# Attention's values as seven products of halves, with tokens on partitions and most moving parts kept on chip

## The chip, the core and the metric

The kernel runs on one core of a Trainium2 chip. The metric is device time in microseconds, the median over runs; one more execution is recorded by the profiler, and its time is given beside the median. The engines are called PE (TensorE), DVE (VectorE), ACT (ScalarE), POOL (GpSimd) and SP (SyncE).

## What is computed

One layer over 512 tokens of width 2048, in float32. A normalised input `h = rmsnorm(x)` is multiplied by a wide matrix; the columns of the product are queries, keys, values and gates of two mixers:

```python
h = rmsnorm(x, norm_gain)
proj = h @ w_in
(aq, ak, av, az, iq, ik, iw, rq, rk, rv, rz, ga, gb) = split(proj)
a_out = dsa_mixer(aq, ak, av, iq, ik, iw, positions, rel_bias) * silu(az)     # top-k attention, 8 heads of 128
b_out = retention_mixer(rope(rq), rope(rk), rv, ret_gn_gain) * silu(rz)       # 8 heads of 128
merged = sigmoid(ga) * (a_out @ w_a_out) + sigmoid(gb) * (b_out @ w_b_out)
r = x + merged @ w_o
y = rmsnorm(r + (p @ w_ple) * sigmoid(r @ w_ple_gate), final_gain)
```

The change is in `av`, the values of the attention: 512 tokens x 1024 columns, a sum over 2048.

## The kernel before

The order of all work is written out by hand: one Python program issues instructions to the engines' queues, and a queue runs in the order in which it was filled. What is wanted later is put off with `later(n, f)`, by `n` ticks of `step()`, a call that stands behind every few matmuls. `todo` holds work for the next ticks, and `bg` work for the background, of which one item is taken every `state["rate"]` ticks when `todo` is empty.

A float32 operand is used as two parts, high and low: ACT rounds the high part (`L137` for weights), DVE subtracts it for the low part (`L142`). A product takes three matmuls: high x high, high x low, low x high.

Weights arrive through `raw` (a DMA of 512 KB into one of seven `wraw` buffers) and `units` (one split into `wh` and `wl`, three buffers of each). `split_to` and `load_to` run ahead of the matmuls by `AHEAD` = 3 and `LOADS` = 5 units more. Most projections are computed in pairs by `gemm_pair`: two outputs of 128 channels, the sum over 2048 cut in two halves, tokens cut in two halves, so that seven products of half blocks replace eight (the scheme of Strassen in Winograd's form). Its seven weight combinations come from DMAs that add to a buffer (`add_block`, on POOL's queue) and one addition on DVE (`L144`). Its seven moving combinations, `PRODUCTS` = s3, a11, a12, s4, s2, a22, s1, have eight row blocks each: 56 tiles of 128 x 512 (256 high and 256 low columns). `combos` builds them, four steps for each row block `k`; a step rounds on ACT and subtracts on DVE. The 56 tiles are built in the background, stored to `hd` in memory, and loaded back later.

The stages that matter here, in order:

- The index scores, whose queries are the first projection. Row block 0 of the moving parts is begun here.
- `values(u_rv[i], "rv")`, retention's values: tokens are on the output's partitions, `hparts` (32 tiles: 16 row blocks of `h` in two parts) are the stationary operand, and weights of 512 columns move. Each of the two calls has 16 row blocks x 4 token tiles x 3 matmuls. In the background, at one item in two ticks, the moving parts are built.
- `values(u_av[i], "av")`, attention's values, in the same form, with the weights in 16 units of two row blocks. In the background are the 48 top-k rounds (`MAX8` and `MATCH_REPLACE8` on DVE), one in three ticks. Here `x_load` brings the 56 tiles back, while `hparts` are freed. The result is scaled by `R["nat"]`, split and stored to `vd`.
- 24 gate pairs: eight retention heads, each one `gemm_pair` for its query and key and two for gates. In the background, at one item in 18 ticks, are the masks of the position bias.
- The pairs of the other projections, attention, the output projections and the end.

On chip, 69 tiles of 128 x 512 (`U`), five of 128 x 1280 (`B`) and eight PSUM banks (`P`) are handed out.

Of the kernel before, what the change touches and what calls it, by code (L numbers as in the profile page):

```python
# [35 lines left out]
def block_kernel(tc, xT, pT, posb, posq, w_in, w_v, w_ik, w_a, w_b, w_o, w_ple, w_gate,  # L36
# [4 lines left out]
    with contextlib.ExitStack() as ctx:  # L41
# [10 lines left out]
        def U(name, dt=F32):  # L52
            return up.tile([128, L], dt, name=name, tag="u")
# [17 lines left out]
        raw_tiles = {}  # L71
        unfinished = {}
        state = {"raw": 0, "split": 0, "rate": BG_RATE}
        in_raws = set()

        def raw(src, k0, nk, cols, plus=None):
            raws.append((src, k0, nk, cols, plus))
# [2 lines left out]
        def block(src, chunks, cols=128):  # L80
            ids, k0 = [], 0
            for nk in chunks:
                ids.append(len(units))
                units.append((raw(src, k0, nk, cols), None, nk, cols))
                k0 += nk
            return ids

        def block_pair(s1, s2):
# [8 lines left out]
                units.append((r, plus, 8, 128))  # L97
            return list(range(first, first + 7))

        def view(t, nk, cols):  # L100
            return t.rearrange("p a c -> p (a c)")[:, 0:nk * cols].rearrange("p (a c) -> p a c", c=cols)

        def add_block(r, b):
            src, k0 = b
            pool.dma_start(out=raw_tiles[r], in_=src[:, k0:k0 + 8, :], accum_op=OP.add)  # L105
# [53 lines left out]
        def later(n, f):  # L159
            if n <= 0:  # L160
                return f()
            tick[1] += 1
            heapq.heappush(soon, (tick[0] + n, tick[1], f))
# [108 lines left out]
                if ended[n] == 16 and n in after:  # L272
                    after[n]()

        def combos(lo, hi, name, keep=None):


            X = {n: [None] * 8 for n in PRODUCTS}
            T = {}

            def parts(n, k, src, sign=1.0):
                t = U(name + n, F32R)
                act.activation(t[:, LO], src, AF.Copy, scale=sign)
                if sign > 0:
                    dve.tensor_sub(t[:, HI], src, t[:, LO].bitcast(F32))
                else:
                    dve.scalar_tensor_tensor(t[:, HI], src, sign, t[:, LO].bitcast(F32), op0=OP.mult, op1=OP.subtract)
                if keep is None:
                    X[n][k] = t
                else:  # L290
                    later(6, lambda: sp.dma_start(keep(n, k), t.bitcast(F32)))
# [33 lines left out]
        u_rv, u_av = ([block(w_v[i], (2,) * 8, 512) for i in g] for g in ((0, 1), (2, 3)))  # L325
        u_r, u_g = [], []
        for h in range(NH):
            u_r.append(block_pair(col(RQ, h), col(RK, h)))
# [345 lines left out]
            for b, ps in [(b, bias_mm(b)) for b in banks]:  # L674
                bias_out(b, ps)

        hd = dp.tile([56, 128, L], F32, name="hd")
        x_at = {(n, k): hd[8 * i + k] for i, n in enumerate(PRODUCTS) for k in range(8)}
        xn = {}

        def xn_load(k):
# [178 lines left out]
        Xh = {n: [None] * 8 for n in PRODUCTS}  # L860
        x_wanted = collections.deque((n, k) for n in PRODUCTS for k in range(8))

        def x_load(count):
            while x_wanted and count:
# [3 lines left out]
                count -= 1  # L868

        for i in range(2):  # L870
            for t, ps in enumerate(values(u_rv[i], "rv")):
                act.dma_start(rd[i, t], normal(ps, "rv", t))
        for i in range(2):
            pss = values(u_av[i], "av", lambda s, i=i: x_load(2 if i else 1 + s % 2))
            vs = [normal(ps, "av", t, F32 if t == NT - 1 else F32R) for t, ps in enumerate(pss)]
            for t in range(NT - 1):
                vl = U("avl", F32R)
                dve.scalar_tensor_tensor(vl, pss[t], R["nat"][:, t:t + 1], vs[2 * t].bitcast(F32), op0=OP.mult,
                                         op1=OP.subtract)
                vs.insert(2 * t + 1, vl)  # L880
            for j, v in enumerate(vs):
                later(8 + (6 if i else 2) * j, lambda v=v, j=j, i=i: act.dma_start(vd[i, j], v if j == 6 else v.bitcast(F32)))
# [30 lines left out]
        state["rate"] = BG_RATES[3]  # L913
        for n, u in enumerate(u_rz):
            y = B("y2")

# [402 lines left out]
AHEAD = 3  # L1319
LOADS = 5  # L1320
BG_RATE = 4
BG_RATES = (2, 3, 18, 9)
HEAD = 13
WARM = 10
MANUAL = True
# [96 lines left out]
```

## Time and profile before

| what | value |
|---|---|
| median of three runs | 1683.71 us (1683.71 to 1684.24) |
| the profiled execution | 1684.08 us, of which the span is 1682.3 us |
| granted TensorE clock | 0.998 |
| PE, weight loads, DVE, ACT, POOL busy | 99%, 86%, 76%, 51%, 13% of the span |
| DMA | 355.85 MB, 212 GB/s over the span |
| values of retention | from 95.7 us; of attention, from 192.1 to 279.1 us |

In the profile, a group of instructions is shown by its line, its engine and operation, what it writes and reads, how often it ran, its busy time and the mean of one in ns, and then the idle time of the engine just before it and what ended that. PEld are the weight loads of PE. A matmul's end is modelled, and matmuls overlap.

### The profile page before, as it was taken

To read this page: it belongs to the slowest core of one execution; us is meant where nothing else is said; L and a number is where in the kernel's file an instruction comes from. 1 tells how busy PE (TensorE), PEld (TensorE's weight loads), DVE (VectorE), ACT (ScalarE), POOL (GpSimd) and SP (SyncE) were. 2 spreads that over 40 slices of the span, in tenths; PEclk is the share of its full clock that TensorE was granted. 3 is DMA by queue.
4 is the path that set the end of the run, shared out by engine and by line. 5 is a ranking of instruction groups with operands and counts; after the bars stand their busy time and mean duration, and the time that the engine had idled before them with its cause. 6 is when DMAs were issued, how large, how long until landed. Compare 5 with 4: busy or idle time off the path is not lost.

```text
span 1682.3 us, 24757 instructions
## 1 busy us (share of the span) xinstructions
PE 1669.6 (99%) x9208; PEld 1450.9 (86%) x9208; DVE 1275.8 (76%) x2020; ACT 864.8 (51%) x1278; POOL 216.4 (13%) x216
## 2 busy tenths in 40 slices
PE   9999999999999999999999999999999999999997
PEld 7988888888888888888888888888888888888896
DVE  7797888988888888877877876787668877864453
ACT  7465423555565555555555555566634444463342
POOL 2100000111111111111331111100000111112222
PEclk9999999999999999999999999999999999999999
DMA  7438989788788788788988888998566788733222
GB/s 289 126 107 308 374 296 337 176 228 218 187 225 207 200 215 212 199 213 212 254 237 221 214 206 232 242 361 292 173 202 191 194 224 214 209 112 100 88 63 100
DMA packets 135368, 355.85 MB, mean 212 GB/s; under 512 B 14800, under 2 KB 26960, under 8 KB 135248
## 3 DMA queue, kind: packets, MB, share of 16 engines
q1 hardware_dynamic: 102496, 256.20, 44.4%
q0 software_dynamic: 21376, 77.60, 25.4%
q10 hardware_dynamic: 11376, 20.47, 3.3%
q8 instruction: 72, 1.18, 0.3%
q14 instruction: 48, 0.39, 0.1%
HBM read 301.26 MB, written 52.95 MB: 211 GB/s over the span
## 4 chain that ended last, share of the span: by engine, by line
PE 95%; DVE 2%; ACT 1%; issue 1%; DMA 0%; POOL 0%; SPq 0%; POOLq 0%; DVEq 0%; ACTq 0%
PE ps_p L267 24%; PE ps_v L267 16%; PE ps_r L267 8%; PE ps_q L267 8%; PE ps_vn L734 3%; PE ps_vn L735 3%; PE ps_vn L736 3%; PE ps_w L198 3%; PE ps_w L197 3%; PE ps_w L199 3%; PE ps_pg L199 3%; PE ps_pg L197 3%; PE ps_pg L198 3%; PE ps_iq L197 1%; PE ps_iq L199 1%; PE ps_iq L198 1%
## 5 line engine op out<-in xcount | busy, mean ns | idle before, releaser
L142 DVE TENSOR_TENSOR wl<-wraw,wh 128x1024 fp32r<-128x1024 f32 (+2 forms) x459 | 560.0, 1231 | 186.3 <-ACT wh L137 184.3
L137 ACT ACTIVATE wh<-wraw 128x1024 fp32r<-128x1024 f32 (+2 forms) x459 | 474.4, 1043 | 305.4 <-DVE wraw L144 133.8
L105 POOL DMA_DIRECT2D wraw<-w_in x120 | 106.1, 957 | 833.7 <-DVE wl L142 262.5
L230 ACT ACTIVATE e<-ps_p 128x512 f32<-128x512 f32 x144 | 86.1, 598 | 146.9 <-PE ps_p L267 142.4
L267 PE MATMUL ps_p<-hs,wh 128*128 128x512 f32 x640 | 161.3, 394 | 0.0
L267 PEld LDWEIGHTS ps_p<-hs,wh 128*128 128x128 f32 x640 | 114.9, 189 | 21.2 <-issue 0.7
L734 PE MATMUL ps_vn<-wh,hh 128*128 128x512 f32 x256 | 99.8, 390 | 0.0
L735 PE MATMUL ps_vn<-wl,hh 128*128 128x512 f32 x256 | 99.7, 390 | 0.0
L736 PE MATMUL ps_vn<-wh,hl 128*128 128x512 f32 x256 | 99.7, 389 | 0.0
L267 PE MATMUL ps_p<-hs,wl 128*128 128x256 f32 x640 | 92.0, 284 | 0.0
L267 PEld LDWEIGHTS ps_p<-hs,wl 128*128 128x128 f32 x640 | 83.0, 192 | 0.5 <-issue 0.4
L267 PE MATMUL ps_v<-ha,wh 128*128 128x512 f32 x320 | 80.6, 393 | 0.0
L267 PE MATMUL ps_q<-ha,wh 128*128 128x512 f32 x320 | 80.1, 392 | 0.0
L267 PE MATMUL ps_r<-hs,wh 128*128 128x512 f32 x320 | 79.2, 389 | 0.4 <-ACT wh L137 0.4
L267 PE MATMUL ps_v<-hs,wh 128*128 128x512 f32 x320 | 79.5, 390 | 0.0
L267 PE MATMUL ps_p<-ha,wh 128*128 128x512 f32 x320 | 79.2, 390 | 0.0
L199 PE MATMUL ps_pg<-rh,wl 128*128 128x512 f32 x192 | 74.8, 390 | 0.0
L197 PE MATMUL ps_pg<-rh,wh 128*128 128x512 f32 x192 | 74.7, 389 | 0.0
L198 PE MATMUL ps_pg<-rl,wh 128*128 128x512 f32 x192 | 74.7, 389 | 0.0
L895 DVE TENSOR_TENSOR go<-e_t 128x256 f32<-128x256 f32 x160 | 68.0, 425 | 5.6
L267 PEld LDWEIGHTS ps_r<-hs,wh 128*128 128x128 f32 x320 | 60.0, 188 | 13.3 <-ACT wh L137 0.8
L267 PEld LDWEIGHTS ps_p<-ha,wh 128*128 128x128 f32 x320 | 60.0, 188 | 12.9 <-issue 0.4
(361 smaller groups left out, 3500.5 us busy)
## 6 DMA issues: line engine op xcount, KB each, us to landing
wraw<-w_in SPq DMA_DIRECT2D x172, 512.0 KB, 5.5
wraw<-w_in POOLq DMA_DIRECT2D x120, 512.0 KB, 8.0
wraw<-w_v SPq DMA_DIRECT2D x32, 512.0 KB, 4.9
wraw<-w_o SPq DMA_DIRECT2D x32, 512.0 KB, 5.0
wraw<-w_o POOLq DMA_DIRECT2D x24, 512.0 KB, 6.1
wraw<-w_gate SPq DMA_DIRECT2D x24, 512.0 KB, 3.9
hd<-hs SPq DMA_DIRECT2D x32, 256.0 KB, 4.9
hs<-hd SPq DMA_DIRECT2D x32, 256.0 KB, 5.4
```

Source lines behind the costliest of these rows:

```text
L105: pool.dma_start(out=raw_tiles[r], in_=src[:, k0:k0 + 8, :], accum_op=OP.add)
L137: act.activation(h, raw, AF.Copy)
L142: dve.tensor_sub(l, raw, h.bitcast(F32))
L197: pe.matmul(o, h[:, k, w], a, start=(s == order[0]), stop=False)
L198: pe.matmul(o, h[:, k, w], b, start=False, stop=False)
L199: pe.matmul(o, l[:, k, w], a, start=False, stop=(s == order[-1]))
L230: act.activation(E[n], src, AF.Copy)
L267: pe.matmul(o[:, c], w[:, k], X[PRODUCTS[n]][k][:, c], start=(n < 4 and first and k == 0), stop=(ended[n] == 16), skip_group_check=True)
L734: pe.matmul(pss[t], a[:, tok(t)], h[:, k], start=(s == 0), stop=False)
L735: pe.matmul(pss[t], a[:, tok(t)], l[:, k], start=False, stop=False)
L736: pe.matmul(pss[t], b[:, tok(t)], h[:, k], start=False, stop=(s == KT - 1))
L895: dve.tensor_add(o[:, q], c0, c1)
```

## The change

Attention's values take the form of `gemm_pair`, but with tokens on the output's partitions. The moving combinations become the stationary operand, 128 tokens at a time (columns `tok(j)` hold a high part, `tok(2 + j)` its low part), and the weight combinations move, 512 columns wide. The two outputs are the two blocks of 512 channels. Each of the seven products has eight row blocks x 2 token tiles x 3 matmuls, and the four accumulators take two banks each, all eight.

The weight combinations come from `block_wide_pair`: 20 loads, 16 adds by DMA on POOL's queue, 28 splits. The four `t` tiles lie in `B` buffers, and their first add is put off by 12 ticks.

The moving combinations must therefore be ready before attention's values, and 44 of the 56 stay on chip from when they are built. Twelve (s2, a22 and s1 of row blocks 0 to 3, `X_AWAY` = 4) are still stored and loaded back, now during retention's second call. The sums of `combos` and three of the low parts (s1, s4, a22) are issued on POOL instead of DVE; for the merged tiles later in the kernel, `combos` stays on DVE. The results of the values are not scaled any more, since the moving parts are normalised already.

The background's rates change: one item in five ticks during attention's values, one in 24 for what is left of the top-k rounds in the gate pairs, then one in 16, and later one in eight instead of nine.

```diff
+        def block_wide_pair(s1, s2):
+            ks = range(0, 8, 2)
+            t = [raw(s2, k, 2, 512, (s2, k + 8)) for k in ks]
+            w11, w21, w22 = ([raw(s, k + o, 2, 512) for k in ks] for s, o in ((s1, 0), (s1, 8), (s2, 8)))
+            s = [raw(s1, k, 2, 512, (s2, k)) for k in ks]
+            in_big.update(t)
+            first = len(units)
+            for r, plus in ((t, (s1, 0)), (w11, None), (w21, None), (w22, None), (t, (s1, 8)), (t, None), (s, None)):
+                units.extend((r[n], plus and (plus[0], plus[1] + k), 2, 512) for n, k in enumerate(ks))
+            return [list(range(i, i + 4)) for i in range(first, first + 28, 4)]
...
+                elif i in in_big:
+                    t = B("wt").rearrange("p (a c) -> p a c", c=128)
...
-                    add_block(i, plus)
+                    later(12 if i in in_big else 0, lambda i=i, plus=plus: add_block(i, plus))
...
-        def combos(lo, hi, name, keep=None):
+        def combos(lo, hi, name, keep=None, adder=dve, low={}):
...
-                    dve.tensor_sub(t[:, HI], src, t[:, LO].bitcast(F32))
+                    low.get(n, dve).tensor_sub(t[:, HI], src, t[:, LO].bitcast(F32))
...
-                dve.tensor_sub(t2[:, LO], x[:, LO], x[:, HI])
-                dve.tensor_sub(t1[:, LO], x[:, HI], y[:, HI])
-                dve.tensor_sub(t1[:, HI], x[:, LO], t1[:, LO])
-                dve.tensor_sub(t2[:, HI], y[:, LO], t1[:, HI])
+                adder.tensor_sub(t2[:, LO], x[:, LO], x[:, HI])
+                adder.tensor_sub(t1[:, LO], x[:, HI], y[:, HI])
+                adder.tensor_sub(t1[:, HI], x[:, LO], t1[:, LO])
+                adder.tensor_sub(t2[:, HI], y[:, LO], t1[:, HI])
...
-        _, h_step = combos(lambda k: xn[k], lambda k: xn[k + 8], "h", lambda n, k: x_at[n, k])
+        Xh, h_step = combos(lambda k: xn[k], lambda k: xn[k + 8], "h", lambda n, k: x_at.get((n, k)), pool,
+                            {n: pool for n in ("s1", "s4", "a22")})
...
+        bg.append(lambda: state.update(rate=BG_RATES[4]))
...
-        for i in range(2):
-            pss = values(u_av[i], "av", lambda s, i=i: x_load(2 if i else 1 + s % 2))
...
+        def value_out(i, t, f, x, y):
+            a = U("av")
+            f(a, x, y)
+            if t == NT - 1:
+                vs = [(6, a)]
+            else:
+                h, l = split(a, "av", 2)
+                vs = [(2 * t, h.bitcast(F32)), (2 * t + 1, l.bitcast(F32))]
+            for j, v in vs:
+                later(10 + 2 * (j % 2), lambda j=j, v=v: act.dma_start(vd[i, j], v))
...
+            after = {
+                0: lambda: copy("pv", "v"),
+                1: lambda: copy("e1", "p"),
+                2: lambda: out(dve.tensor_sub, "q", "e1", 0, 0),
+                4: lambda: copy("e2", "p"),
+                5: lambda: out(dve.tensor_sub, "v", "e2", 0, 1),
+                6: last,
+            }
+            for n, b in enumerate("vpqrpvp"):
...
+                for s, (i, k) in enumerate(seq):
+                    if k == 0:
+                        split_to(i + AHEAD)
+                        load_to(i + AHEAD + LOADS)
+                    h, l = loaded[i]
+                    x = Xh[PRODUCTS[n]][s]
+                    for j in range(2):
+                        a, c = x[:, tok(j)], x[:, tok(2 + j)]
+                        o = banks[b][j]
+                        pe.matmul(o, a, h[:, k], start=(n < 4 and s == 0), stop=False, skip_group_check=True)
+                        pe.matmul(o, a, l[:, k], start=False, stop=False, skip_group_check=True)
+                        pe.matmul(o, c, h[:, k], start=False, stop=(s == 7), skip_group_check=True)
+                        step()
+                if n in after:
+                    after[n]()
...
-BG_RATES = (2, 3, 18, 9)
+BG_RATES = (2, 3, 5, 24, 16, 8)
+X_AWAY = 4
```

More of the change, by code (lines that the diff above doesn't have):

```diff
@@ L73, in block_kernel @@
         state = {"raw": 0, "split": 0, "rate": BG_RATE}
-        in_raws = set()
+        in_raws, in_big = set(), set()
         def raw(src, k0, nk, cols, plus=None):
@@ L104, in add_block @@
             src, k0 = b
-            pool.dma_start(out=raw_tiles[r], in_=src[:, k0:k0 + 8, :], accum_op=OP.add)
+            _, _, nk, cols, _ = raws[r]
+            pool.dma_start(out=view(raw_tiles[r], nk, cols), in_=src[:, k0:k0 + nk, :], accum_op=OP.add)
         def load_to(n):
@@ L284, in parts @@
                 if sign > 0:
-                    dve.tensor_sub(t[:, HI], src, t[:, LO].bitcast(F32))
+                    low.get(n, dve).tensor_sub(t[:, HI], src, t[:, LO].bitcast(F32))
                 else:
                     dve.scalar_tensor_tensor(t[:, HI], src, sign, t[:, LO].bitcast(F32), op0=OP.mult, op1=OP.subtract)
-                if keep is None:
+                dst = keep and keep(n, k)
+                if dst is None:
                     X[n][k] = t
                 else:
-                    later(6, lambda: sp.dma_start(keep(n, k), t.bitcast(F32)))
+                    later(6, lambda: sp.dma_start(dst, t.bitcast(F32)))
             def sums(k):
@@ L324, in block_kernel @@
         u_iq = [None, None] + [block(col(IQ, m), K8) for m in range(2, 8)]
-        u_rv, u_av = ([block(w_v[i], (2,) * 8, 512) for i in g] for g in ((0, 1), (2, 3)))
+        u_rv = [block(w_v[i], (2,) * 8, 512) for i in range(2)]
+        u_av = block_wide_pair(w_v[2], w_v[3])
         u_r, u_g = [], []
@@ L675, in bias_banks @@
                 bias_out(b, ps)
-        hd = dp.tile([56, 128, L], F32, name="hd")
-        x_at = {(n, k): hd[8 * i + k] for i, n in enumerate(PRODUCTS) for k in range(8)}
+        x_away = [(n, k) for k in range(X_AWAY) for n in PRODUCTS[4:]]
+        hd = dp.tile([len(x_away), 128, L], F32, name="hd")
+        x_at = {nk: hd[i] for i, nk in enumerate(x_away)}
         xn = {}
@@ L858, in retention, with x_load @@
             return rotate
[L860 to L864, printed above, removed]
+        x_wanted = collections.deque(x_away)
+        def x_load(s):
+            if s >= KT - len(x_away) and x_wanted:
                 n, k = x_wanted.popleft()
@@ L867, in x_load @@
                 sp.dma_start(Xh[n][k].bitcast(F32), x_at[n, k])
-                count -= 1
         for i in range(2):
-            for t, ps in enumerate(values(u_rv[i], "rv")):
+            pss = values(u_rv[i], "rv", x_load if i else lambda s: None)
+            for t, ps in enumerate(pss):
                 act.dma_start(rd[i, t], normal(ps, "rv", t))
-        for i in range(2):
-            pss = values(u_av[i], "av", lambda s, i=i: x_load(2 if i else 1 + s % 2))
[L875 to L882, printed above, removed]
@@ L883, in block_kernel, with values_pair, copy, out @@
-        state["rate"] = BG_RATES[2]
+        state["rate"] = BG_RATES[2]
+        def value_out(i, t, f, x, y):
[8 more added lines that the diff above has]
+                later(10 + 2 * (j % 2), lambda j=j, v=v: act.dma_start(vd[i, j], v))
+        def values_pair(ids):
+            banks = {}
+            E = {}
+            def copy(n, b):
+                E[n] = [U(n) for _ in range(2)]
+                for j in range(2):
+                    act.activation(E[n][j], banks[b][j], AF.Copy)
+            def out(f, b, n, i, half):
+                for j in range(2):
+                    value_out(i, 2 * half + j, f, banks[b][j], E[n][j])
+            def last():
+                copy("e3", "p")
+                out(dve.tensor_sub, "p", "pv", 1, 1)
+                out(dve.tensor_add, "r", "e3", 1, 0)
+            after = {
[7 more added lines that the diff above has]
+            for n, b in enumerate("vpqrpvp"):
+                if b not in banks:
+                    banks[b] = [P("ps_v" + b) for _ in range(2)]
+                seq = ksteps(ids[n])
+                for s, (i, k) in enumerate(seq):
[4 more added lines that the diff above has]
+                    x = Xh[PRODUCTS[n]][s]
+                    for j in range(2):
+                        a, c = x[:, tok(j)], x[:, tok(2 + j)]
[6 more added lines that the diff above has]
+                    after[n]()
@@ L886, in block_kernel @@
+        values_pair(u_av)
+        state["rate"] = BG_RATES[3]
         sgb, sga, mbs = (dp.tile([16, 128, L], F32, name=n) for n in ("sgb", "sga", "mbs"))
```

2 lines of the change are left out of this document (1 added, 1 removed).

## The prediction

> **What bounds the kernel now.** I read the page first: the busy shares, then the chain that ended last.
>
> ```profile
> span 1682.3 us, 24757 instructions
> ...
> PE 1669.6 (99%) x9208; PEld 1450.9 (86%) x9208; DVE 1275.8 (76%) x2020; ACT 864.8 (51%) x1278; POOL 216.4 (13%) x216
> ...
> PE 95%; DVE 2%; ACT 1%; issue 1%; DMA 0%; POOL 0%; SPq 0%; POOLq 0%; DVEq 0%; ACTq 0%
> ```
>
> TensorE (PE) is 95% of the chain, so matmuls removed from it are worth their time unless something else comes late. Busy time does not say what a matmul is worth: a matmul is booked from its own start to its modelled end, and neighbours overlap. The timeline gives the pace. It shows the first matmuls of attention's values and the first one after them:
>
> ```profile
> 192.09 0.39 PE L734 MATMUL ps_vn<-wh,hh 128*128 128x512 f32 x1
> 192.32 0.39 PE L735 MATMUL ps_vn<-wl,hh 128*128 128x512 f32 x1
> 192.55 0.39 PE L736 MATMUL ps_vn<-wh,hl 128*128 128x512 f32 x1
> 192.77 0.39 PE L734 MATMUL ps_vn<-wh,hh 128*128 128x512 f32 x1
> ...
> 279.13 1.98 PE L267 MATMUL ps_v<-hs,wh 128*128 128x512 f32 x8
> ```
>
> Each is booked 0.39 us, but three start every 0.68 us. The stage is 2 outputs x 16 row blocks x 4 token tiles x 3 = 384 matmuls in 279.13 - 192.09 = 87.04 us: 0.2267 us each, and 0.2267 is the price used below. Next the stages around it, in the table by windows (columns: length, then busy time of PE, weight loads, DVE, ACT, POOL, granted clock, DMA share, GB/s):
>
> ```profile
> 130.00:192.10 62.10, 62.10 (x276) 51.41 (x275) 52.76 (x114) 34.34 (x69) 0.00 (x0) 1.00 0.95 346
> 192.10:235.60 43.50, 43.50 (x193) 36.03 (x192) 33.22 (x72) 11.70 (x13) 0.00 (x0) 1.00 0.91 329
> 235.60:279.10 43.50, 43.50 (x193) 36.04 (x192) 34.76 (x77) 11.09 (x13) 3.73 (x4) 1.00 0.96 327
> 279.10:342.60 63.50, 62.96 (x371) 55.31 (x370) 56.11 (x91) 34.91 (x45) 7.41 (x8) 1.00 0.80 210
> 406.10:469.60 63.50, 63.50 (x388) 55.76 (x387) 52.33 (x80) 35.07 (x46) 9.95 (x10) 1.00 0.80 205
> ```
>
> The first row is the retention values with seven of the eight steps that build the moving parts; then the two halves of attention's values; then two groups of three gate pairs. PE never waits in the first three although the DMA share reaches 0.96, and DVE is near 80 to 88% throughout. So the question is what the change does to DVE and to arrivals, not to PE alone.
>
> **The matmuls removed.** Seven products x 8 row blocks x 2 token tiles x 3 matmuls = 336 take the place of 384; the instruction list of the new program has 9104 entries on PE instead of 9152, which is the same 48. Form, stationary 128 columns and moving 512 columns are as before, in triples on one bank. 48 x 0.2267 = **10.88 us** saved if PE stays dense; the stage becomes 76.2 us.
>
> **The weights.** There are 28 splits instead of 16, and a unit (two row blocks) lasts 12 x 0.2267 = 2.72 us on PE instead of 5.44.
>
> ```profile
> L142 DVE TENSOR_TENSOR wl<-wraw,wh 128x1024 fp32r<-128x1024 f32 x16 | 19.6, 1225 | 17.9 <-ACT wh L137 17.9
> L137 ACT ACTIVATE wh<-wraw 128x1024 fp32r<-128x1024 f32 x17 | 18.0, 1060 | 58.8 <-PE ps_vn L736 49.6 <-DMA wraw<-w_v 4.4 <-DVE m L632 4.4
> L633 DVE MATCH_VALUE_LOAD isc<-m,isc 128x8 f32 x43 | 4.0, 92 | 1.5
> L878 DVE SCALAR_TENSOR_TENSOR avl<-ps_vn,r_nat,av 128x512 fp32r<-128x512 f32 x6 | 4.1, 745 | 0.0
> L234 DVE TENSOR_TENSOR e_t<-ps_q,e 128x512 f32<-128x512 f32 x48 | 33.0, 688 | 11.2 <-PE ps_q L267 10.8
> ```
>
> DVE in the new stage: 28 x 1.225 = 34.3 us of splits. A top-k round: the two half-stages hold 33.22 + 34.76 - 19.6 - 4.1 = 44.3 us for 43 rounds, 1.03 each; at one in five steps of 112 that is 22 rounds, 22.7 us. Outputs: 8 sums and 6 low parts at 0.69, 9.7 us. Together 66.7 of 76.2 us, 88%: full, but not over. ACT has 28 x 1.06 + 8 copies and 6 high parts of about 0.65, 39 of 76. With three split buffers the split of unit i+2 starts when PE starts unit i, takes 1.06 + 1.23 = 2.29 us and is due after 5.44: **3.15 us of slack**, against 8.6 before. The burst after a product (two sums, 1.38 us, then two low parts) fits in it. At the end of the stage four sums (2.8 us) stand on DVE ahead of the next gate pair's third split, whose low part is due only after six runs of eight matmuls. I take 0.2 us for this joint, bounds 0 and 2 (a store still holding the slot of an output).
>
> **The moving parts.** 44 of 56 stores and loads go, off SP's queue: nobody on PE waited for them (DMA 0% of the chain), so nothing is gained. Seven of each step's 256-wide subtractions go from DVE to POOL: 4 sums and 3 low parts. ACT waits for POOL's sums before it can round them, and the next weight split is queued behind that on ACT; DVE's own low parts wait for the same. On POOL's queue the adds of weights by DMA stand between them. The prices:
>
> ```profile
> L285 DVE TENSOR_TENSOR hs<-t,hs 128x256 fp32r<-128x256 f32 x29 | 10.7, 416 | 0.0
> ...
> L1306 POOL TENSOR_TENSOR yo<-y,b 128x128 f32<-128x128 f32 x3 | 1.3, 455 | 1.7 <-ACT b L1300 1.7
> ...
> 1524.59 1.29 POOL L381 TENSOR_TENSOR sq<-sq 128x512 f32<-128x512 f32 x1 [41.40 <-ACT sq L376]
> ...
> 39.28 5.55 POOL L381 TENSOR_TENSOR sq<-sq 128x512 f32<-128x512 f32 x3 [8.74 <-ACT sq L376]
> ...
> 40.18 3.50 DVE L381 TENSOR_TENSOR sq<-sq 128x512 f32<-128x512 f32 x2
> 43.60 2.31 DVE L142 TENSOR_TENSOR wl<-wraw,wh 128x1024 fp32r<-128x1024 f32 x1
> 45.84 0.68 DVE L381 TENSOR_TENSOR sq<-sq 128x512 f32<-128x512 f32 x1
> ```
>
> No 256-wide subtraction on POOL is in the trace; between 0.455 (128) and 1.29 us (512) lies 0.73. The last four rows are the warning: while POOL runs, DVE slows. From 40.18 to 45.84 DVE did 2 x 0.69 + 1.23 = 2.6 us of work in 5.66: three POOL instructions cost it 3.06 us, 79% of their own 3 x 1.29. So the two engines nearly take turns. In the first window 49 subtractions move: DVE keeps 52.76 - 49 x 0.416 = 32.4 us, POOL gets 49 x 0.73 = 35.8. At 79% the two need 32.4 + 28.3 = 60.7 of 62.1 us, no backlog; at 100%, 68.2, a backlog of 6.1 us where values begin. What exceeds the slack of 3.15 stops PE: 0 to 3 us. I take **1.3 us**.
>
> The Trainium skill (GPSIMD Engine Reference, Engine selection) speaks against the move: elementwise work of two inputs belongs on VectorE, GpSimd being about twice as slow. The rows agree (0.73 against 0.416); by the page's factor 1.96 a subtraction is 0.82 us, an estimate, and POOL's total 40 instead of 35.8 us, still under the window's 62.1.
>
> **The adds by DMA.** The new stage needs 16 adds of 512 KB on POOL's queue and 20 plain loads, where it had 16 loads.
>
> ```profile
> q1 hardware_dynamic: 102496, 256.20, 44.4%
> q0 software_dynamic: 21376, 77.60, 25.4%
> ...
> DMA to landing us min/median/max: 5.3/7.8/12.5
> ```
>
> A plain 512 KB takes 0.444 x 1682.3 / 489 = 1.53 us of all 16 DMA engines, an add 0.254 x 1682.3 / 148 = 2.89. The first four loads and adds, and the next four adds, spread over the retention stage. The tight place is units 15 to 26: the four t tiles are added to again right after their second split and split again four units later (10.9 us), and four s adds and the next gate pair's first add stand in the same queue: 9 x 2.89 + 3 loads (4.6) + 4 stores of half the size (3.1) = 33.7 us of transfers in 11.2 units = 30.5 us. So the last ones run 3.2 us behind, where, with 7.8 us to land, about 2.9 us are spare. I take **0.5 us**, bounds 0 and 7 (every add at the 12.5 us maximum, and the gate pair's adds pushed behind). ACT is the waiter: the split waits for the add, and the bank copies queue behind it.
>
> **The background.**
>
> ```profile
> L648 DVE TENSOR_SCALAR mk<-relf,thr 128x512 f16<-128x512 f32 x22 | 10.6, 480 | 0.0
> ```
>
> The top-k rounds left (about 21) now go into nine gate pairs, one in 24 steps: 7 rounds per group of 168 steps, 7.2 us, in place of about 9 masks at 0.48, 4.5 us. DVE goes from 52.33 to 55 of 63.5 us. The group at 279.10 had 56.11 and PE idled 0.54 us there; so 0 to 0.5 a group. I take 0.4 in all.
>
> **Sum.** The profiled execution took 1684.08 us (span 1682.3, 1.8 around it). 1684.08 - 10.88 + 1.3 + 0.5 + 0.2 + 0.4 = 1675.6; the median of the runs stands 0.4 below the profiled one, so **1675.2 us**. With no stall it is 1672.8.
>
> **Rivals.**
>
> *POOL takes its turns whole* (slower). If each POOL subtraction costs DVE what POOL shows under contention, 5.55 / 3 = 1.85 per 512, so 0.93 per 256, the first window needs 32.4 + 45.3 = 77.7 of 62.1 us, 15.6 over; the step before it adds 7 x (0.93 - 0.416) = 3.6. Backlog 19.2, less 3.15 of slack: 16.0 us of stall, 1684.08 - 10.88 + 16.0 - 0.4 = 1688.8. It decides from a backlog of about 17.5 us. For it: the 2.31 us split above. Against: the same rows put the cost at 79% of 1.29, and part of DVE's remaining time is idle. 0.10. The Trainium skill (SBUF — State Buffer, SBUF: two separate sides) states this turn-taking: a GpSimd instruction and a VectorE one with two SBUF inputs exclude each other for the whole instruction. By that rule the two add up in full; the 79% says a part of POOL's instruction lies outside.
>
> *The adds are late.* The queue of units 15 to 26 slips by 5 to 10 us and ACT stands on it, stopping PE at products five to seven and at the first gate pair: 1678 to 1684. For it: 33.7 us of transfers in 30.5. Against: windows with a DMA share of 0.95 cost PE nothing. 0.15.
>
> *The background hurts.* DVE at 87% in nine gate pairs delays splits by some 0.8 us a pair: 1680 to 1682. For it: the 0.54 us idle at 56.11. Against: that is all it cost. 0.07.
>
> *Nothing is saved:* excluded, the instruction list is 48 matmuls shorter on a bound engine. Other surprises, either way: 0.03.
>
> **How the numbers follow.** The forecast, 1672.8 to 1679, has 0.65. A measurement of this kernel cannot tell less than about 0.2% (3.4 us) from no change: faster means below 1680.3, slower above 1687.1. Faster: 0.65, two thirds of the late adds, half of the background: 0.78; a little less, 0.76, for surprises. Slower: the turns and some surprises, 0.11. Same: 0.13. The range 1672.4 to 1682.5 leaves out the turns and the worst of the adds.
>
> **What would show it.** Right: values in about 76 us with triples every 0.68 us; POOL subtractions near 0.73 to 0.93 us; DVE's splits longer than 1.23 beside them, yet PE without a gap before the first product. Wrong: PE waiting on wl or wh at the start of the values (turns), on wh behind an add at products five to seven (adds), or gate groups longer than 63.5 us (background).

## The result, and the profile after

| | before | after |
|---|---|---|
| median | 1684.01 us (1683.41 to 1686.16, 22 runs) | 1681.87 us (1678.04 to 1685.04, 22 runs) |
| ratio | | 0.9986, 95% interval 0.9979 to 0.9992 |
| profiled execution (span) | 1684.08 us (1682.3) | 1680.43 us (1678.7) |
| mean granted clock of the runs | 0.997 to 0.999 (runs of before beside the experiments) | 0.995 to 0.998 |

The kernel gained 2.1 us where 8.7 were forecast, and its runs spread over 7 us, where those of before spread over 3. The page of the changed kernel, in the same three parts as before:

```profile
span 1678.7 us, 24639 instructions
...
PE 1660.2 (99%) x9160; PEld 1441.5 (86%) x9160; DVE 1300.1 (77%) x1984; ACT 880.0 (52%) x1296; POOL 284.3 (17%) x288
...
PE 89%; DVE 4%; ACT 2%; issue 2%; POOL 2%; DMA 1%; ACTq 0%; SPq 0%; POOLq 0%; DVEq 0%
```

The 48 matmuls are gone (9208 to 9160). But PE carries 89% of the chain instead of 95%, and what it lost went to DVE, ACT and POOL: PE now waits for someone. The table of PE's waits (what waits, for what: us in total, times, longest), of before and then of after (without those of the first 10 us, which are alike), says for whom:

```profile
PE ps_b L1296 <- POOL rl L1292: 3.5, 1, 3.5
PE ps_r L267 <- ACT wh L137: 0.4, 1, 0.4
```

```profile
PE ps_b L1368 <- POOL rl L1364: 3.5, 1, 3.5
PE ps_p L283 <- DVE wl L158: 1.6, 2, 1.3
PE ps_vv L948 <- DVE wl L158: 1.5, 2, 0.8
PE ps_vv L947 <- ACT wh L153: 1.4, 1, 1.4
PE ps_r L283 <- ACT wh L153: 1.3, 3, 0.6
```

New are the waits of `ps_vv`, the first product of the values, and of `ps_p` in the gate pairs; that of `ps_r` there went from 0.4 to 1.3 us. In the timeline, where a stop is the distance between a matmul and its predecessor less their usual pace, there are eight stops: 0.96, 1.54 and 0.93 us in the first product (195.9 to 201.3), 1.46 in the first gate pair (284.5), and 0.80, 0.44, 0.56 and 0.50 in later ones. They add up to 7.2 us; before had 0.87 in this stretch. The span went down by 3.6 us: 10.9 saved, 6.3 of new stops, and 1.0 more that no single stop shows; where that 1.0 went stays open.

The windows of the retention stage and of the two halves of the new stage (columns as in the prediction):

```profile
130.00:192.00 62.00, 62.00 (x276) 51.31 (x275) 54.21 (x57) 31.19 (x63) 49.37 (x52) 1.00 0.84 272
192.00:232.00 40.00, 37.07 (x161) 29.81 (x160) 32.40 (x54) 22.36 (x29) 6.40 (x8) 1.00 0.89 275
232.00:272.00 40.00, 40.00 (x178) 33.10 (x178) 33.26 (x56) 17.36 (x19) 8.69 (x10) 1.00 0.95 227
272.00:335.50 63.50, 61.57 (x366) 54.23 (x365) 57.31 (x95) 35.55 (x47) 8.63 (x10) 1.00 0.83 216
```

Read the first row against that of before. DVE has half the instructions, 57 instead of 114, and is busy for longer, 54.21 instead of 52.76 us. The 57 that left (53 of them such subtractions, 47 moved to POOL) had cost about 57 x 0.416 = 23.7 us; those that stayed now take some 24 to 25 us more. POOL's 47 subtractions, 45 us as booked, cost DVE about 55% of their own time. One takes 1.02 us in the mean over all 56, and 0.84 to 1.13 by group, where 0.73 was worked out. Three of the six groups:

```profile
L301 POOL TENSOR_TENSOR hs<-t,hs 128x256 fp32r<-128x256 f32 x16 | 17.1, 1084 | 17.7 <-ACT hs L299 17.7
L313 POOL TENSOR_TENSOR t<-xn 128x256 f32<-128x256 f32 x8 | 9.1, 1131 | 50.9 <-DVE xn L707 50.9
L301 POOL TENSOR_TENSOR ha<-xn,ha 128x256 fp32r<-128x256 f32 x8 | 7.7, 962 | 0.0
```

And PE loses its 3 us right behind, in the second window. The timeline shows how (a choice of its rows):

```profile
187.22 1.80 DVE L158 TENSOR_TENSOR wl<-wt,wh 128x1024 fp32r<-128x1024 f32 x1 [0.58 <-ACT wh L153]
189.72 0.42 ACT L299 ACTIVATE ha<-xn 128x256 fp32r<-128x256 f32 x1 [2.53 <-DVE xn L707]
190.27 1.75 DVE L303 SCALAR_TENSOR_TENSOR ha<-xn,ha 128x256 fp32r<-128x256 f32 x1
191.81 0.81 POOL L315 TENSOR_TENSOR t<-xn,t 128x256 f32<-128x256 f32 x1
192.65 0.42 ACT L299 ACTIVATE hs<-t 128x256 fp32r<-128x256 f32 x1 [0.47 <-POOL t L315]
192.98 1.04 ACT L153 ACTIVATE wh<-wt 128x1024 fp32r<-128x1024 f32 x1
194.23 0.40 ACT L299 ACTIVATE ha<-xn 128x256 fp32r<-128x256 f32 x1
194.54 0.67 ACT L764 ACTIVATE rv<-ps_vn,r_nat 128x512 f32<-128x512 f32 x1
195.86 0.50 PE L948 MATMUL ps_vv<-wl,hs 128*128 128x512 f32 x1 [0.79 <-DVE wl L158]
197.87 0.69 ACT L764 ACTIVATE rv<-ps_vn,r_nat 128x512 f32<-128x512 f32 x1 [0.48 <-POOL hs L301]
198.97 2.01 ACT L153 ACTIVATE wh<-wt 128x1024 fp32r<-128x1024 f32 x2 [0.40 <-ACT rv L764]
200.07 0.50 PE L947 MATMUL ps_vv<-wh,hs 128*128 128x512 f32 x1 [1.38 <-ACT wh L153]
```

One DVE subtraction of 256 columns takes 1.75 us instead of 0.42, ACT waits for DVE's `xn` and POOL's `t`, and ACT's part of the last step of the moving parts ends at 194.6, when the values have been running for 2.6 us (POOL's last low part ends at 198.5). On ACT's queue, behind these parts, stand the four copies `rv` of the stage before, each followed by the issue of a store, and behind those the third weight split, at 198.97. PE needs it at 198.5.

### The profile page after: what moved, and what is told of

Same layout as the page of the kernel before. It is cut to its first block, busy times and chain, and to the rows that moved or that the text cites. A ratio compares the mean times of both kernels' runs of the same rounds, so it can differ in the third digit from the quotient of the medians.

```text
span 1678.7 us, 24639 instructions
## 1 busy us (share of the span) xinstructions
PE 1660.2 (99%) x9160; PEld 1441.5 (86%) x9160; DVE 1300.1 (77%) x1984; ACT 880.0 (52%) x1296; POOL 284.3 (17%) x288
## 4 chain that ended last, share of the span: by engine, by line
PE 89%; DVE 4%; ACT 2%; issue 2%; POOL 2%; DMA 1%; ACTq 0%; SPq 0%; POOLq 0%; DVEq 0%
PE ps_p L283 23%; PE ps_v L283 15%; PE ps_r L283 8%; PE ps_q L283 7%; PE ps_w L213 3%; PE ps_w L214 3%; PE ps_w L215 3%; PE ps_pg L215 3%; PE ps_pg L213 3%; PE ps_pg L214 3%; PE ps_iq L213 1%; PE ps_iq L215 1%; PE ps_iq L214 1%; DVE wl L158 1%; ACT wh L153 1%
## 5 line engine op out<-in xcount | busy, mean ns | idle before, releaser
L119 POOL DMA_DIRECT2D wraw<-w_o x24 | 21.1, 945 | 348.5 <-DVE wl L158 316.5
L283 PEld LDWEIGHTS ps_v<-hs,wh 128*128 128x128 f32 x320 | 60.1, 188 | 12.5
L283 PEld LDWEIGHTS ps_v<-ha,wh 128*128 128x128 f32 x320 | 59.5, 188 | 12.1
```

What stands on the lines that cost most here:

```text
L119: pool.dma_start(out=view(raw_tiles[r], nk, cols), in_=src[:, k0:k0 + nk, :], accum_op=OP.add)
L283: pe.matmul(o[:, c], w[:, k], X[PRODUCTS[n]][k][:, c], start=(n < 4 and first and k == 0), stop=(ended[n] == 16), skip_group_check=True)
```

## Experiments

Two theories of the first product's stop were set against each other. **A**: it is ACT's queue, where copies and issues of stores stand ahead of the weight splits. **B**: it is DVE and POOL slowing each other while the moving parts are built. In every comparison the kernel before ran on the same chip (medians 1683.55 to 1684.01); the experiments from the spread stores to the stops put in by hand were on another chip than the rest.

**One part undone: the sums.** The subtractions go back to DVE.

```diff
-        Xh, h_step = combos(..., lambda n, k: x_at.get((n, k)), pool, {n: pool for n in ("s1", "s4", "a22")})
+        Xh, h_step = combos(..., lambda n, k: x_at.get((n, k)))
```

> The changed kernel with the sums and all low parts of the moving parts back on DVE, nothing else. In the changed kernel PE stops 3.4 us in the first product of the values: 1.0 us at the split of its second unit, 2.5 us at the third and around it. Theory A (ACT's queue: the third unit's split stands behind the last step of the moving parts and the four copies of retention's values with their stores): only the first part goes, the 2.5 us stay, and the median moves by less than 1.5 us. Rival B (DVE and POOL taking turns is what makes the moving parts late): the whole 3.4 us go and the time falls by about 3 us. If DVE is too full without POOL's help, PE stops longer than 3.4 us and the time rises.

Measured: 1677.42 us (1675.61 to 1681.04), ratio 0.9962 (0.995 to 0.9975). No stop is left in the first product, although the copies are where they were:

```profile
193.36 0.69 ACT L763 ACTIVATE rv<-ps_vn,r_nat 128x512 f32<-128x512 f32 x1 [0.40 <-ACT rv L763]
195.16 2.01 ACT L153 ACTIVATE wh<-wt 128x1024 fp32r<-128x1024 f32 x2 [1.11 <-DMA ha<-hd]
```

The last copy starts at 193.36 instead of 197.87, since ACT's last part of the moving tiles ends at 189.3 instead of 194.6, and the split at 195.16 is in time. So B is needed for the stop, and A alone does not make it.

**The other part: the split ahead of the copies,** with the sums on POOL.

```diff
+            if i:
+                split_to(u_av[0][0] + AHEAD)
             for t, ps in enumerate(pss):
                 act.dma_start(rd[i, t], normal(ps, "rv", t))
```

> The changed kernel with the split of the third unit of the values put on ACT's queue ahead of the four copies of retention's values. Theory A: PE's stop in the first product falls from 3.4 to about 1 us (what is left is the second unit's split), the time falls by 2 to 2.5 us. Rival B: the moving parts hold the queues anyway, PE's stop stays above 2.5 us and the time within 0.7 us.

Measured: 1679.14 us (1677.68 to 1681.31), ratio 0.9971 (0.996 to 0.9981). Stops of 0.95 and 0.94 remain in the first product, 1.9 instead of 3.4 us. So 1.5 us of it is POOL's delay handed on by ACT's queue, and 1.9 us comes from the splits' low parts on DVE directly. The second of the two stops shows it:

```profile
196.28 3.01 DVE L158 TENSOR_TENSOR wl<-wt,wh 128x1024 fp32r<-128x1024 f32 x1
196.47 1.03 POOL L301 TENSOR_TENSOR hs<-t,hs 128x256 fp32r<-128x256 f32 x1
197.18 1.02 POOL L301 TENSOR_TENSOR ha<-xn,ha 128x256 fp32r<-128x256 f32 x1
```

The low part that takes 1.22 us elsewhere takes 3.01 beside POOL's last two subtractions: here DVE pays 1.8 us for the 1.7 us in which they run. Its high part was ready at 195.28; a top-k round stood ahead of it on DVE. In this profile the stop of the first gate pair is longer, 2.56 us.

**The stores of the values from SP's queue,** alone and together with the split ahead.

```diff
-                later(10 + 2 * (j % 2), lambda j=j, v=v: act.dma_start(vd[i, j], v))
+                later(10 + 2 * (j % 2), lambda j=j, v=v: sp.dma_start(vd[i, j], v))
```

> The changed kernel with the 14 stores of the values issued by SP instead of ACT. Theory C (at the first gate pair ACT stands for 3.4 us on the issue of seven stores, and a bank copy and two splits queue behind it): the stops of 1.5 and 0.8 us in the first gate pair go, the time falls by 1.5 to 2.3 us. Rival D (DVE is simply too full in the gate pairs, with top-k rounds beside the outputs): the stops stay, the time moves by less than 0.7 us.

> Both edits, split first and stores on SP. If A and C hold and add up: 4 to 5 us below the changed kernel, about 1677; if the stops are only handed on to the next late thing, less than 2.5 us.

Measured: 1681.6 us (1680.77 to 1683.34) alone, which is nothing gained; 1679.12 (1678.35 to 1680.94) with the split ahead, no better than that without. The stop in the first gate pair goes, so it was ACT held by the stores that it issues. In its place come stops of 0.78, 0.87 and 0.94 us in product six, where ACT waits for the last adds of the `t` tiles (those issued behind their split in product five):

```profile
259.11 1.06 ACT L153 ACTIVATE wh<-wt 128x1024 fp32r<-128x1024 f32 x1 [3.94 <-DMA wt<-w_v]
260.22 0.50 PE L947 MATMUL ps_vv<-wh,ha 128*128 128x512 f32 x1 [0.70 <-ACT wh L153]
```

On SP's queue the stores stand ahead of loads of weights: seven loads that the changed kernel issues from 217 to 236 us are issued from 233 to 237, behind the first four stores. The price forecast for late adds (0.5 us) was not paid in the changed kernel, but it was near.

**Sums on DVE, with SP stores, and with loads asked for earlier.**

```diff
-                        load_to(i + AHEAD + LOADS)
+                        load_to(i + AHEAD + LOADS + 4)
```

> Sums and low parts on DVE and the stores of the values on SP. With the sums on DVE PE had no stop in the first product; with the stores on SP it had none in the first gate pair, but three of 0.6 to 0.9 us at products six and seven, where ACT waited 2.5 to 4.6 us for adds by DMA. Theory E (the adds of units 15 to 26 are at their limit, one issue in 2.45 us on POOL's queue, and PE reaches them earlier when nothing stops it before): the stops at products six and seven are there again, 1.5 to 3 us in sum, and the time is within 1.5 us of the kernel with the sums on DVE alone (1677.4). Rival F (it was the stores' own traffic on SP in one run): no such stops, and the time is about 1675.

> Sums on DVE, and in the values the loads, with the first add of the s tiles, put four units earlier into the queues, so that on POOL three of the four s adds stand ahead of or between the second adds of the t tiles. Theory E: ACT waits less for adds in products six and seven; the stops in the first gate pair (2.1 and 0.8 us) come from ACT's stores and stay, so the time is 1676 to 1678. Rival F: no change beyond 0.5 us, and no change in ACT's waits for adds.

> Sums on DVE, loads four units earlier, stores on SP: all three causes taken away. If the three explain the loss, PE has no stop over 0.6 us before 340 us, and the time is 1673 to 1675, the 10.9 us of the matmuls less what the top-k rounds cost in the gate pairs (0.4 to 0.6 us a group). If not, it stays above 1676.

Measured: SP stores 1677.85 us (1676.26 to 1684.48), no different from ACT stores. The stops in product six are there again (0.53, 0.87 and 0.93 us), as theory E has it, but its reason fails: with the stores on ACT, PE gets there earlier still and does not stop. Loads four units earlier took 1688.53 (1683.46 to 1694.77), and both 1690.11 (1688.82 to 1696.72): slower than before, which neither theory expected. Loads asked for earlier were not issued earlier (the last at 224.5, 228 and 232 us with and without); the last two adds of the `t` tiles were issued 5 us later (243.6 and 248.6 instead of 238.4 and 243.0), and the stores behind them became later. Of the run with early loads:

```profile
257.16 1.06 ACT L153 ACTIVATE wh<-wt 128x1024 fp32r<-128x1024 f32 x1 [5.27 <-DMA wt<-w_v]
281.59 0.63 ACT L733 ACTIVATE avh<-av 128x512 fp32r<-128x512 f32 x1 [5.18 <-DMA vd<-av]
286.94 3.30 PE L283 MATMUL ps_r<-hs,wh 128*128 128x512 f32 x7 [4.74 <-ACT wh L153]
```

ACT stands 5.27 us for an add, and 5.18 us for a slot of an output that a store still holds; the second stops PE for 4.9 us.

**POOL's sums in the kernel before.** Only the move of the sums and low parts is made there.

> The kernel before with the change's move alone: the four sums and three low parts of the moving parts on POOL. Here a unit lasts 5.4 us and a split has 8.6 us of slack. If turns with POOL cost PE only where slack is short, the time is that of before within 0.1%, though DVE's splits beside POOL take longer than 1.23 us. If POOL's work costs by itself, it is slower by 2 us or more.

Measured: 1684.06 us (1683.16 to 1684.66), ratio 1.0 (0.9992 to 1.0009). POOL is busy 46.89 us of the same 62, and DVE 52.79, so the engines hinder each other as much as in the changed kernel; but a unit there lasts 5.44 us on PE, and no split is late. POOL's work costs nothing by itself: it costs in the new stage alone, 0 us here against 4.5 there (1681.87 against 1677.42). That the cut of the slack, worked out as 8.6 to 3.15 us, makes the difference is argued; the moving parts are also due earlier there.

**The stores spread,** with the sums on DVE.

```diff
-                later(10 + 2 * (j % 2), lambda j=j, v=v: act.dma_start(vd[i, j], v))
+                later(10 + 2 * (j % 2) + 6 * (t % 2) + 12 * (i * (t < 2)), lambda j=j, v=v: act.dma_start(vd[i, j], v))
```

> Sums and low parts back on VectorE, and the stores of attention's values put off one after another (6 steps apart) instead of four or seven at the same step. With the sums back on VectorE alone, TensorE stopped 2.12 us in the first gate pair and 0.81, 0.44, 0.58 and 0.52 later. Theory: the first of these is ScalarE held by the burst of stores that it issues at the end of the stage (three in 3.51 us); spread, they leave it free, the 2.12 us go, and the time is 1684.0 - 10.9 + 2.35 = 1675.5, with a mean clock of 0.998. Rival: the four output sums on VectorE hold the split there; then the stop stays near 2.1 and the time near 1677.4.

Measured: 1675.62 us (1673.94 to 1682.92), ratio 0.9954 (0.9941 to 0.9968). The 2.12 us are gone. In the changed kernel the same place reads:

```profile
278.32 2.81 ACTq L906 DMA_DIRECT2D vd<-avl  x3
281.18 0.60 ACT L246 ACTIVATE pv<-ps_v 128x512 f32<-128x512 f32 x1 [3.38 <-DVE wl L158]
284.52 1.22 PE L283 MATMUL ps_p<-hs,wl 128*128 128x256 f32 x8 [1.30 <-DVE wl L158]
```

Three issues of stores keep ACT from 278.3 to 281.1; the copy of the bank, the next high part and PE follow. The row of the copy names DVE, which had been done for long; it was the issues ahead of it on ACT.

**The background slowed in the gate pairs** (`BG_RATES[3]` 48 instead of 24), on top of the spread stores.

> As the run with the spread stores, but in the gate pairs one top-k piece in 48 steps instead of 24. Theory that the background is what stops TensorE by 0.4 to 0.8 us in the later gate pairs: most of the 2.35 us go, 1673.3 to 1674. Rival: those stops come from the retention head's own chain (ScalarE's copies rb that wait for VectorE's go, ahead of the next high part); then they stay and the time is that of the other run, 1675.5. The top-k pieces left over run in the last gate pairs at one in 8, which could give up to 1 us back there.

Measured: 1684.62 us (1680.46 to 1688.8), outside both expectations. The first nine gate pairs take 183.0 us, against 183.1 with the rate of 24 (in the run with the `rd` stores moved, below), with stops of 0.21, 0.88 and 0.18 us against 0.71 and 0.44. So the top-k rounds are not what stops PE there. The stop waits for a high part that stands on ACT's queue behind a retention head's two copies, which wait for DVE:

```profile
297.49 0.63 ACT L785 ACTIVATE rb<-go 64x512 f32<-64x512 f32 x1 [2.63 <-DVE go L966]
298.79 1.06 ACT L153 ACTIVATE wh<-wraw 128x1024 fp32r<-128x1024 f32 x1
299.90 1.42 PE L283 MATMUL ps_r<-hs,wh 128*128 128x512 f32 x5 [0.71 <-ACT wh L153]
```

The profiled execution is 9.1 us longer than that of the run with the `rd` stores moved. By the end of the values it is 3.6 behind, mostly from a stop at 200 us; at 1030 us 1.8 (with 32 more matmuls of the position bias, 1.1 us, still to do), at 1098 us 8.7. In that last stretch stand 64 matmuls of the position bias:

```profile
1079.03 5.36 PE L677 MATMUL ps_bias<-mk,d 128*32 128x128 f16 x64
1079.18 4.78 DVE L666 TENSOR_SCALAR mk<-relf,thr 128x128 f16<-128x128 f32 x24
```

In the other run the same 64 take 1.08 us. Here the slower background had left 24 of their masks unmade, and DVE makes them while PE waits for one after the other, though PE is booked as busy: 4.3 us. Right behind, from 1083.9 to 1087.3, the granted clock is 0.50, and the run falls back by another 1.2 us (from 7.2 to 8.4). With the 3.6 these make up the 9.1. The stop at 200 us is a finding of its own:

```profile
194.59 0.69 ACT L763 ACTIVATE rv<-ps_vn,r_nat 128x512 f32<-128x512 f32 x1 [0.82 <-DMA hs<-hd]
198.53 0.33 ACTq L891 DMA_DIRECT2D rd<-rv  x1
198.90 2.00 ACT L153 ACTIVATE wh<-wt 128x1024 fp32r<-128x1024 f32 x2 [3.62 <-DMA ha<-hd]
200.01 0.51 PE L946 MATMUL ps_vv<-wh,hs 128*128 128x512 f32 x1 [1.68 <-ACT wh L153]
```

```profile
194.00:199.00 5.00, 4.33 (x20) 3.25 (x18) 0.00 (x0) 0.79 (x2) 0.00 (x0) 1.00 1.06 322
```

The copy ends at 195.28, and its store is issued at 198.53, 3.2 us later (3.4 and 4.2 us in the two runs with DVE's sums and SP stores). The wait of the split behind it is put down to the landing of a load, and in these 5 us (second fence, columns as in the windows above) the DMA share is 1.06; meanwhile ACT does nothing else. With equal code up to there, the run with the spread stores alone issued it 0.8 us after the copy, and the kernel before 0.03 us after. So it varies from run to run.

**Stops put in by hand, in the kernel before.** The low part of four units is computed 10 or 12 times over.

```diff
-                    dve.tensor_sub(l, raw, h.bitcast(F32))
+                    for _ in range(10 if i in (u_av[0][2], u_av[0][6], u_av[1][2], u_av[1][6]) else 1):
+                        dve.tensor_sub(l, raw, h.bitcast(F32))
```

> The kernel before with four stops of TensorE put in by hand: in attention's values the low part of four units is worked out ten times in a row (same values). Nine more of 1.225 us are 11.0 us, less 8.6 of slack: a stop of about 2.4 us each, 9.7 in all. Theory: a stop of 2 us or more can be followed by some 3.4 us at half the granted clock, which costs 1.7 us more; then the time is 1684 + 9.7 + up to 6.8 = 1694 to 1700.5 and the mean clock 0.994 to 0.997, and it differs from run to run. Rival: the lower clock of some runs has nothing to do with the stops; then 1693.7 and a clock of 0.998.

> The same with twelve low parts in a row: 13.5 us less 8.6, four stops of about 4.9 us, 19.5 in all. Theory: every stop of this length brings at least 3.4 us at half clock: 1684 + 19.5 + 6.8 = 1710 or a little more (the half clock may last longer than one such stretch), mean clock 0.992 to 0.994, in every run. Rival (clock apart from the stops): 1703.5 at 0.998.

Measured: 1710.92 us (1710.55 to 1711.1) and 1722.13 (1721.57 to 1723.39). The stops were longer than worked out, 5.15, 4.59, 5.59 and 4.31 us, since top-k rounds stand ahead of the splits and the true slack was about 6 us. Their sum is 19.6; the kernel lost 27.0. The windows around the first one (columns: length, PE busy, granted clock, DMA share, GB/s) show the rest:

```profile
200.00:204.00 4.00, 2.76 (x13) 1.00 0.92 340
204.00:208.00 4.00, 0.26 (x1) 0.66 0.75 286
208.00:212.00 4.00, 4.00 (x10) 0.50 0.78 243
212.00:216.00 4.00, 4.00 (x18) 0.98 0.88 283
```

The granted clock falls to 0.50 while PE stands, and stays there for 4 us after PE is back: 10 matmuls in 4 us instead of 18. Each of the eight stops is followed by such a stretch, about 3.4, 6.8 or, once, 10.2 us long, which begins 2.6 to 5.1 us after PE stopped; 7.3 us of loss behind four stops is 1.8 each, and with the longer stops (28.7 in all) 9.5 us, 2.4 each. The same half clock stands in other traces behind stops that came by themselves: after 2.05 us (with 0.92 more), 2.44, 2.56, 3.21, 4.91 and 6.83 us; after one of 2.12 us it did not come.

Where a stop falls seems to decide. In all these traces the stretches at 0.50, and the times between them, are multiples of 3.41 us (up to the last 40 us of a run). Cut into pieces of that length, counted from a change of the clock, 15 of the 16 stretches begin right behind a piece in which PE, as booked, stood idle for 1.65 to 3.41 us; the other one is that behind the 64 waiting matmuls. Of the pieces at full clock that are not followed by one, none has more than 1.70 us. The stop of 2.12 us lay across a border, with 1.70 us in one piece; that of 2.56 us had 2.04 in one.

**Everything that ACT issues around the values, moved.** The stores are spread and SP issues the four `rd` stores of the second retention output; once with the sums on DVE, once with the sums on POOL and the split ahead, once with all of it.

```diff
-                act.dma_start(rd[i, t], normal(ps, "rv", t))
+                (sp if i else act).dma_start(rd[i, t], normal(ps, "rv", t))
```

> Sums and low parts on VectorE, stores of attention's values spread, and the four stores of the second retention output issued by SyncE instead of ScalarE. Theory: the stop that some executions show near 200 us (1.7 to 3 us, TensorE waiting for wh) is ScalarE standing at the issue of the fourth such store, 3.2 us after its copy had ended, with the weight split behind it; off ScalarE it is gone in every run: 1673.5 to 1675.5 and no run above 1678, clock 0.998. Rival: the split waits for a transfer of its own (an add of weights that lands late); then the stop still comes in some runs, spread and median as with the spread stores alone (1675.6, up to 1683).

> The changed kernel with its sums and low parts still on GpSimd, but the two kinds of stores as above and the first weight split put ahead of the four copies. Theory: of the 3.4 us in the first product, 1.9 are VectorE and GpSimd in each other's way and stay, the joint at the first gate pair (1.5 us) and the clock's share go: 1676.5 to 1678. Rival: all of it was ScalarE's queue (copies and store issues ahead of the splits), and GpSimd's sums cost nothing: 1674 to 1675.5.

> All of it: sums and low parts on VectorE, both kinds of stores moved, first split ahead of the copies. Theory: nothing is left but the 2 us of short stops in the gate pairs, 1673.5 to 1675, as without the split put ahead. Rival: the split ahead of the copies holds the banks longer and gives back 0.5 to 1 us.

Measured: **1674.53 us** (1674.18 to 1676.58), ratio 0.9947 (0.9934 to 0.9959), the fastest of all; 1677.27 (1676.73 to 1680.29), ratio 0.9964 (0.9952 to 0.9977); 1676.06 (1674.17 to 1676.55), ratio 0.9953 (0.994 to 0.9967). Of the first:

```profile
190.29 2.73 ACT L763 ACTIVATE rv<-ps_vn,r_nat 128x512 f32<-128x512 f32 x4 [0.72 <-PE ps_vn L756]
192.92 1.05 ACT L153 ACTIVATE wh<-wt 128x1024 fp32r<-128x1024 f32 x1
```

The four copies run without a pause, and the split comes at 192.92, 6 us earlier than in the run with the slower background. No run of the five was above 1676.6, as the theory had it. What is left there are 2.2 us of stops in the gate pairs. The split ahead adds nothing to this. With POOL's sums, 0.95 and 0.94 us remain in the first product, as expected of B, and the median is 2.7 us above the first and 1.2 above that with the same split ahead; the intervals overlap, but the stops in the traces are told apart.

## Why the prediction was off

**The matmuls** (10.9 us): right. With most stops taken away, the kernel takes 1674.5 us with 2.2 us of stops left, where 1672.8 was forecast for none.

**DVE and POOL** (1.3 us, bounds 0 and 3): the mechanism was right, the size was not. A POOL subtraction took 1.02 us in the mean where 0.73 was worked out, and DVE paid about 55% of it rather than 79%; ACT's part of the moving tiles ended 5.3 us later than without POOL, near the upper end of the backlog (6.1). The step that failed is the next one. The slack of 3.15 us was compared with the backlog as if only the splits stood behind it. On ACT's queue four copies and four stores stood there too, and no term had them; on DVE a top-k round can stand ahead of a split, which the slack leaves out (for before, 8.6 us was worked out in the same way, and the stops put in by hand show about 6). So the first product lost 3.4 us, 1.9 on DVE and 1.5 through ACT. The rival in which POOL takes its turns whole (16 us of stall) is refuted as a sum, though the low part of 3.01 us paid POOL's time in full.

**The joint** (0.2 us, bounds 0 and 2): 1.46 us in the profile, 2.12 with the sums on DVE. The working looked at DVE's four sums; the cause was ACT, which issues the stores (three issues in 2.81 us). The cost of an issue on ACT appears in no term.

**The adds** (0.5 us): no stop in products five to seven. They had little room to spare, though: SP stores, or loads asked for earlier, bring such stops at once.

**The background** (0.4 us): 2.3 us of stops in the gate pairs, 0.87 of which before had too. Half the rate did not take them away, so this term had the wrong cause: what PE waits for there is a high part behind a retention head's copies on ACT. These stood there before too; why they cost more now is not shown.

**What was missing: the clock.** Terms for stops were summed as if a stop costs its length. One of 2 us or more can be followed by 3.4 us at half clock, 1.7 us more. For the stops put in by hand this is shown, and the run with the split ahead, whose code at the joint is that of the changed kernel, has it there: half clock from 283.3 to 286.7 us behind the stop of 2.56. For the changed kernel's own slower runs it is argued: its runs at a mean clock of 0.998 took 1678.0 to 1680.9 us and those at 0.995 took 1683.7 to 1685.0, and 0.001 of mean clock is 3.4 us at half. Its profiled execution was one at 0.998 with no half clock in this stretch, so no trace shows its slower runs. The Trainium skill (TensorE: Matmul & The Clock Gate, What's actually happening) states such a gate, which halves the clock after at least one idle window of about 3.4 us that runs freely. The 0.50 and the length of 3.4 us agree; that stops of 2.05 to 2.56 us were followed by it shows that less idle time can do.

In sum, the median lay 6.7 us above the forecast. In the profiled execution the terms were too small by 2.1 (DVE and POOL), 1.3 (the joint) and 1.0 us (the background), the adds too large by 0.5, and 1.0 is in no term; the rest is that the median lies 1.4 above the profiled execution, where 0.4 below was forecast. Moving the issues and the split on ACT takes off 4.6 (1681.87 to 1677.27: 1.5 in the first product, 1.5 at the joint; that the rest went with the clock is argued). Moving the sums back to DVE as well takes off another 1.2 (to 1676.06), and without the split ahead 2.7 (to 1674.53); with five runs each, the last two are not told apart.

## What to carry to other kernels

When a stage gets shorter on the bound engine, list everything that stands in the queues of the engines that feed it, copies and issues of DMAs too, and not only the operations that the change touches: slack that covered them is gone. Work moved from one engine to another can slow what stays, and so relieve nothing, as 47 subtractions did here; compare busy time, not counts. And a stop of the bound engine can cost more than its length: here those of 2 us and more were mostly followed by half clock, and single stops of up to 1.8 us were not, so one stop of 3 us is worse than several short ones that lie apart.

## What was not expected of the hardware

- 47 subtractions moved from DVE to POOL left DVE's busy time as it was (52.76 to 54.21 us in 62, with 57 instructions instead of 114).
- A 256 KB store was issued on ACT 3.2 us after its data were ready, at a DMA share of 1.06, with ACT idle meanwhile; in another run of the same code it was 0.8 us.
- The granted clock was 0.50 for about 3.4, 6.8 or 10.2 us behind each of eight stops of 4.3 to 7.7 us, and behind some of 2.05 to 2.56 us.
